# A two-layer hybrid decoder step: quartered first loads on two queues, a shorter table stage, small loads behind the weights, attention squares block by block

## The chip, the cores and the metric

One NeuronCore of a Trainium2 chip. Its engines work side by side and wait for each other by semaphores: TensorE (PE, matrix products), VectorE (DVE), ScalarE (ACT), GpSimd (POOL) and SyncE (SP, which here issues DMAs). The metric is the device time of one launch in microseconds (us), all inputs in the chip's memory; smaller is better.

## The reference

One inference step of two layers on 256 prompt tokens and 64 sample tokens (8 sequences of 8), all in fp32, model width 1024:

```python
x = x + 0.5 * swiglu(rms_norm(x, lw['ffn1_norm']), lw['ffn1_w_gate'], lw['ffn1_w_up'], lw['ffn1_w_down'])
mix, new_k, new_v, h_last = token_mixer(rms_norm(x, lw['mix_norm']), lw, h0, cache_k, cache_v)
x = x + mix
x = x + 0.5 * swiglu(rms_norm(x, lw['ffn2_norm']), lw['ffn2_w_gate'], lw['ffn2_w_up'], lw['ffn2_w_down'])
gate = jax.nn.sigmoid((rms_norm(x, lw['ple_norm']) @ lw['ple_w_gate']).astype(F32))
x = x + ((p @ lw['ple_w_proj']).astype(F32) * gate).astype(x.dtype)
```

`swiglu(h) = (silu(h @ w_gate) * (h @ w_up)) @ w_down` with an inner width of 2816. `token_mixer` projects to u, q, k, v; u goes through a state-space recurrence (S5: 32 groups of 16 channels, 64 complex states each, `h_t = Abar h_{t-1} + Bbar u_t`, then gelu and a gate), q, k, v through sliding-window attention with sinks; both results are normalised on their own (`rms_norm`), joined and projected by `w_out`. `Abar` and `Bbar` come from `exp(lam * dt)`. A last `rms_norm` ends the step. Outputs are y, the key/value windows and the final states.

## The kernel before

All 320 tokens stand in the free dimension: x is eight tiles `x[m]` of 128x320 (`xa`). Every fp32 product is made of three fp32r products (`mm3`, L178): the weight is split in a rounded part `wh` and the rest `wl`, the activations likewise in `big` pairs (`Norm.cut`, L218: ACT makes the rounded part L225, DVE the rest L226), and each 128-row step issues h·xh (L182), h·xl (L183) and lo·xh (L184).

**Weights** stream through `wfetch` (L150): SP loads a raw tile of up to 128x1024 (`wr`, 4 buffers), ACT copies it to fp32r (`wh`, L163), DVE subtracts (`wl`, L164); 4 buffers of each, three split weights kept ahead of the matmuls. For the very first weight the load and the cuts are made in two halves (`HEAD`).

**Norms** run late: matmuls work on the unnormalised x times the gain, and the result is scaled by r afterwards. `Norm.stat` makes squares and adds them (ACT L210 or POOL L212; sums by DVE or POOL, L216), `finish` adds over the partitions with three small matmuls (L244), DVE forms the mean `ms` (L247), POOL takes the power -0.5 (L249), and after `LATER` further matmuls PE spreads r over the partitions (L267) and DVE copies it.

**Head.** SP issues two tiles of x, the parameters `prm`, the two halves of the first gate weight, three tiles of x, the first up weight, three tiles of x, then the next weights. ACT and DVE cut x; POOL and ACT make the squares of all eight tiles. Block m=0 of the first FFN multiplies k-steps 0 to 6 and then 7 (`KCUT`) with either weight; `finish` comes after the third of such groups in general, and after the fifth here (FAFTER), which is m=1's gate product.

**FFN.** The inner width goes in two halves (12 and 10 blocks of 128). Each block m is a gate group into PSUM pool "pc" and an up group into "pt", 24 matmuls each; then eight down-projection blocks `mo` per half, of 36 matmuls with two 768-column weights in the first half and of 30 with two 640-column weights in the second. A second-half block ends with `fd` (L334), the addition to x (L335) and `post`, which cuts x for the next norm, squares it and adds the square.

**Table stage.** `prep(l)` (L378) is a generator of the state-space tables: powers of `Abar`, the B tables (L489, L493; transposed on PE into `wbd`), the C tables (L521, L525; `wcd`, and with matmuls the kernel taps `ktd`, copied into the triangular `ttd`, of which everything is first filled with zeros from a 128x1024 tile, 2 MB a layer, L385), and the tables of powers over chunks `ect`, `est`, `dec` (`er`, `us`, `uc`: L558 to L570; doubling L579 to L584; one step of normalising to modulus one, L590 to L595; L597). `ffn` takes one step of it after each of its 22 blocks and 16 down-projection blocks (`step`, L145), which also waits in program order for the last weight cut and load issued. `prep(0)` runs beside ffn1 of layer 0, `prep(1)` beside ffn2 of layer 0. prep(0) has 36 steps before, prep(1) fewer since its zero fills are prep(0)'s.

**Mix.** The mixer projects, runs the recurrence in chunks and the attention in prompt blocks (`Prompt`, one for each m, results to `ya[:, m, 0:256]`) and sample blocks, in a written-out order; `attn_norm` (L929) makes the four whole squares of `ya` and finishes, `ssm_norm` does the same for the recurrence. The loads of the state h0 (L689) and of the layer's embedding pT (L970) are issued wherever SP is free: at 20.50 and 20.97 us.

Instructions that no data ties together are placed by a scheduler that orders each engine's queue by estimated times; `tc.issue_after(i)` forbids it to place anything in its scope ahead of i.

## Time and profile before

| | |
|---|---|
| median of 3 runs | 1286.86 us (1286.62 to 1287.45) |
| the profiled execution | 1286.57 us |
| its span in the trace | 1284.8 us |
| mean granted clock of TensorE | 0.995 |
| PE busy | 1257.4 us, 98%, 9153 instructions |
| DVE, ACT, POOL busy | 911.0, 598.9, 81.5 us |
| moved by DMA | 210.62 MB, mean 164 GB/s |

All times count from the start of the span; some 1.8 us of the run's time lie around it. "Busy" of PE includes matmuls that run at the throttled clock. "x 9153" counts instructions. An entry such as `PE pt L184 <- DVE wl L164` reads: PE's instruction of line 184 that writes a tile `pt` had to wait for DVE's instruction of line 164 that writes `wl`. Queue rows (SPq) are the issue of a DMA, not its transfer. Matmuls overlap, so a matmul's duration (0.31 us) is longer than its distance to the next.

### The profile page before, as it was taken

How to read it: one execution, taken by the hardware profiler on the slowest of the kernel's cores; microseconds unless marked ns; L12 is line 12 of the kernel's file. 1: busy time of each engine (PE TensorE's matmuls, PEld its weight loads, DVE VectorE, ACT ScalarE, POOL GpSimd, SP SyncE). 2: the span in 40 equal slices, each digit the busy share in tenths (PEclk: the TensorE clock that was granted, in tenths of full speed). 3: DMA queues.
4: the chain of work that ended last, by engine and by line, in shares of the span. 5: the costliest groups of instructions: out<-in, count | busy, mean ns of one | idle time of the engine just before them, and what ended most of it. 6: DMA issues, size and time to landing. Idle time of an engine off the chain costs nothing.

```text
span 1284.8 us, 22994 instructions
## 1 busy us (share of the span) xinstructions
PE 1257.4 (98%) x9153; PEld 1231.1 (96%) x9153; DVE 911.0 (71%) x1609; ACT 598.9 (47%) x984; POOL 81.5 (6%) x96
## 2 busy tenths in 40 slices
PE   7999999899999999999999999999999999999996
PEld 7999999898899999999999999999888999999996
DVE  6588776978786878788785555557877755555575
ACT  5443433455764443344653333345476543333454
POOL 4300002001004000010000000000000000000000
PEclk9999999999999999999999999999999999999998
DMA  7836666354254468654444454345432444454351
GB/s 251 314 125 204 240 208 212 120 197 144 76 192 147 150 194 256 219 189 141 166 174 151 129 154 174 136 115 188 164 106 99 147 151 135 142 180 141 113 174 41
DMA packets 74620, 210.62 MB, mean 164 GB/s; under 512 B 8545, under 2 KB 18497, under 8 KB 74481
## 3 DMA queue, kind: packets, MB, share of 16 engines
q1 hardware_dynamic: 72560, 203.22, 47.8%
q0 software_dynamic: 1664, 5.28, 1.3%
q8 instruction: 72, 1.18, 0.4%
q10 hardware_dynamic: 288, 0.66, 0.1%
q14 instruction: 36, 0.29, 0.1%
HBM read 191.78 MB, written 19.69 MB: 165 GB/s over the span
## 4 chain that ended last, share of the span: by engine, by line
PE 89%; DVE 6%; issue 3%; ACT 1%; POOL 1%; DMA 0%; SPq 0%; POOLq 0%; DVEq 0%; ACTq 0%
PE pt L182 17%; PE pt L184 17%; PE pt L183 17%; PE pc L182 11%; PE pc L184 11%; PE pc L183 11%; DVE wl L164 2%; PE pa L872 1%; PE pa L500 1%; POOL r L249 1%; DVE s L704 0%; DVE s L703 0%; DMA xa<-xT 0%; PE pa L883 0%; PE pa L244 0%
## 5 line engine op out<-in xcount | busy, mean ns | idle before, releaser
L163 ACT ACTIVATE wh<-wr 128x1024 fp32r<-128x1024 f32 (+3 forms) x365 | 350.9, 963 | 556.3 <-issue 302.0
L184 PE MATMUL pt<-big,wl 128*128 128x320 f32 x1584 | 492.6, 311 | 4.3 <-DVE wl L164 4.3
L182 PE MATMUL pt<-big,wh 128*128 128x320 f32 x1584 | 493.4, 312 | 0.0
L183 PE MATMUL pt<-big,wh 128*128 128x320 f32 x1584 | 492.2, 311 | 0.0
L164 DVE TENSOR_TENSOR wl<-wr,wh 128x1024 fp32r<-128x1024 f32 (+3 forms) x365 | 403.1, 1107 | 100.5 <-ACT wh L163 98.5
L182 PE MATMUL pc<-big,wh 128*128 128x320 f32 x992 | 310.7, 314 | 6.7 <-ACT wh L163 6.0
L183 PE MATMUL pc<-big,wh 128*128 128x320 f32 x992 | 308.8, 312 | 0.0
L184 PE MATMUL pc<-big,wl 128*128 128x320 f32 x992 | 308.2, 311 | 0.0
L184 PEld LDWEIGHTS pt<-big,wl 128*128 128x128 f32 x1584 | 298.8, 189 | 6.0 <-DVE wl L164 5.5
L183 PEld LDWEIGHTS pt<-big,wh 128*128 128x128 f32 x1584 | 299.1, 189 | 0.5
L182 PEld LDWEIGHTS pt<-big,wh 128*128 128x128 f32 x1584 | 298.8, 189 | 0.7 <-issue 0.4
L182 PEld LDWEIGHTS pc<-big,wh 128*128 128x128 f32 x992 | 187.2, 189 | 9.6 <-ACT wh L163 6.2
L183 PEld LDWEIGHTS pc<-big,wh 128*128 128x128 f32 x992 | 187.1, 189 | 1.2 <-DVE big L226 1.2
L184 PEld LDWEIGHTS pc<-big,wl 128*128 128x128 f32 x992 | 187.2, 189 | 0.6 <-issue 0.3
L291 DVE TENSOR_TENSOR fa<-pt,ft 128x320 f32<-128x320 f32 x88 | 43.0, 489 | 91.0 <-PE pt L184 90.5
L288 DVE TENSOR_TENSOR ft<-pc,r 128x320 f32<-128x320 f32 x88 | 42.6, 488 | 53.6 <-PE pc L184 53.5
L334 DVE SCALAR_TENSOR_TENSOR fd<-pt,r 128x320 f32<-128x320 f32 x64 | 31.3, 490 | 31.6 <-PE pt L184 31.6
L249 POOL TENSOR_TENSOR r<-ms,mhalf 107x3 f32<-107x3 f32 x13 | 17.1, 1319 | 565.0 <-DVE ms L247 565.0
L225 ACT ACTIVATE big<-xa,prm 128x320 fp32r<-128x320 f32 x64 | 35.3, 559 | 31.4 <-DVE xa L335 17.4
L295 ACT ACTIVATE big<-fa 128x320 fp32r<-128x320 f32 x88 | 40.2, 459 | 14.6 <-DVE fa L291 14.5
L289 ACT ACTIVATE ft<-ft 128x320 f32<-128x320 f32 x88 | 40.0, 458 | 13.1 <-DVE ft L288 13.0
L226 DVE SCALAR_TENSOR_TENSOR big<-xa,prm,big 128x320 fp32r<-128x320 f32 x64 | 37.9, 599 | 8.4 <-ACT big L225 8.4
(246 smaller groups left out, 904.6 us busy)
## 6 DMA issues: line engine op xcount, KB each, us to landing
wr<-f1u SPq DMA_DIRECT2D x44, 512.0 KB, 3.2
wr<-f2g SPq DMA_DIRECT2D x44, 512.0 KB, 3.3
wr<-f2u SPq DMA_DIRECT2D x44, 512.0 KB, 3.3
wr<-f1g SPq DMA_DIRECT2D x43, 512.0 KB, 3.3
wr<-f1d SPq DMA_DIRECT2D x32, 384.0 KB, 3.1
wr<-f2d SPq DMA_DIRECT2D x32, 384.0 KB, 3.1
wr<-f1d SPq DMA_DIRECT2D x32, 320.0 KB, 2.9
wr<-win SPq DMA_DIRECT2D x20, 512.0 KB, 3.8
```

What stands on the lines that cost most here:

```text
L163: S.activation(h[:, c], raw[:, c], AF.Copy)
L164: i = V.tensor_tensor(lo[:, c], raw[:, c], h[:, c].bitcast(F32), op=OP.subtract)
L182: PE.matmul(ps, h[:, c], xh, start=start and k == 0, stop=False)
L183: PE.matmul(ps, h[:, c], xl, start=False, stop=False)
L184: PE.matmul(ps, lo[:, c], xh, start=False, stop=stop and k == n - 1)
L225: S.activation(h, src, AF.Copy, scale=g)
L226: V.scalar_tensor_tensor(lo, src, g, h.bitcast(F32), op0=OP.mult, op1=OP.subtract)
L288: V.tensor_tensor(t, pg, r, op=OP.mult)
L289: S.activation(t, t, AF.Silu)
L291: V.tensor_tensor(a, pu, t, op=OP.mult)
L295: S.activation(h, a, AF.Copy)
L334: V.scalar_tensor_tensor(t, pd, 0.5, r, op0=OP.mult, op1=OP.mult)
```

## The change

1. **Head.** `prm` is loaded first. x comes in quarters of two tiles (three on ACT's queue, the last on SP), and the first gate and up weights in quarters of 256 columns on SP; ACT and DVE cut tile, weight quarters, tile. Block m=0 goes by two k-steps, alternating both weights. Before any data, PE multiplies zeros 14 times (`NWARM`). The squares of x move behind m=0 and from POOL to ACT and DVE. Block m=2 uses the PSUM pool "po" for its gate product.
2. **Table stage.** The chunk tables (`er`, `us`, doubling) come right after the powers, and the normalising to modulus one is applied to the single first column before the doubling. The C tables come next, then the copies to `ttd`, then the B tables. The triangle's zeros are now 112 zero columns of `ktd` (240 wide), so that the copies have one shape and carry the zeros; the 2 MB fills go. prep(0) has 32 steps.
3. **Small loads.** h0 and pT are issued behind the last weight load issued (`later_load`).
4. **Attention squares.** Each prompt block squares its 256 columns and adds them when it is done; the sample columns of all four are squared at the end.
5. `LATER` is 18 instead of 22, and the spread of r may not be placed ahead of the 18th matmul. The `hold` argument of `finish` is not used by any caller.

```diff
-HEAD = 2
-LATER = 22
+NWARM = 14
+LATER = 18
...
+    headdma = []
+    nc.sync.dma_start(prm, I["prm"])
+    for q in range(4):
+        (S if q < 3 else nc.sync).dma_start(xa[:, 2 * q : 2 * q + 2], I["xT"][:, 2 * q : 2 * q + 2])
+        for raw, src in zip(first, firstw):
+            headdma.append(nc.sync.dma_start(raw[:, 256 * q : 256 * q + 256],
+                                             src[:, 256 * q : 256 * q + 256]).ins)
...
+    pz = pst("po")
+    for _ in range(NWARM):
+        PE.matmul(pz[:, :T], zr_[:, :P], zr_, start=True, stop=True)
...
+    def later_load(out, src):
+        with tc.issue_after(lastdma[-1]):
+            nc.sync.dma_start(out, src)
...
             if waiting:
                 waiting[0][0] -= 3
                 if waiting[0][0] <= 0:
-                    waiting.pop(0)[1]()
+                    with tc.issue_after(mm.ins):
+                        waiting.pop(0)[1]()
...
-                    for k0, k1 in ((0, KCUT), (KCUT, 8)):
+                    ks = (0, 2, 4, 6, 8) if head else (0, KCUT, 8)
+                    for k0, k1 in zip(ks, ks[1:]):
...
+                    if head:
+                        groups = 4
+                        for k in range(8):
+                            pre.stat(x[k])
                 else:
-                    for tag in ("pc", "pt"):
+                    for tag in ("po" if head and m == 2 else "pc", "pt"):
...
-            zt = wpool.tile([P, 1024], F32, name=nm("wr"), tag="wr", bufs=4)
-            PO.memset(zt, 0.0)
-            for ll in range(L):
-                nc.sync.dma_start(tt_d[ll].rearrange("p (b c) -> p b c", b=4),
-                                  zt.unsqueeze(1).to_broadcast([P, 4, 1024]))
-                yield
...
+        if l == 0:
+            zt = auxt("sx", [P, 4, 112])
+            PO.memset(zt, 0.0)
+            for ll in range(L):
+                nc.sync.dma_start(kt_d[ll].rearrange("(p b) c -> p b c", b=4)[:, :, 0:112], zt)
+            yield
...
+        V.tensor_tensor(t, uc, uc, op=OP.mult)
+        V.tensor_tensor(er, us, us, op=OP.mult)
+        V.tensor_tensor(t, t, er, op=OP.add)
+        V.tensor_scalar(t, t, -0.5, 1.5, op0=OP.mult, op1=OP.add)
+        V.tensor_tensor(ct_[:, :, 1], uc, t, op=OP.mult)
+        V.tensor_tensor(sn_[:, :, 1], us, t, op=OP.mult)
...
-            PO.dma_start(dst[:, :, i * 16 :], src[:, :, : (8 - i) * 16])
+            PO.dma_start(dst, src[:, :, (7 - i) * 16 : (7 - i) * 16 + P])
...
-        for c0 in (0, 16):
-            cc, ss = ct_[:, :, c0 : c0 + 16], sn_[:, :, c0 : c0 + 16]
-            q1, q2 = auxt("s", [P, G, 16]), auxt("p", [P, G, 16])
-            V.tensor_tensor(q1, cc, cc, op=OP.mult)
-            V.tensor_tensor(q2, ss, ss, op=OP.mult)
-            V.tensor_tensor(q1, q1, q2, op=OP.add)
-            V.tensor_scalar(q1, q1, -0.5, 1.5, op0=OP.mult, op1=OP.add)
-            V.tensor_tensor(cc, cc, q1, op=OP.mult)
-            V.tensor_tensor(ss, ss, q1, op=OP.mult)
...
+        def attn_stat(m):
...
+            if m is not None:
+                sq = na.acc if hold["acc"] else sm.tile([P, T], F32, name=nm("sq"), tag="sq", bufs=2)
+                S.activation(sq[:, 0:TP], ya[:, m, 0:TP], AF.Square)
+                if not hold["acc"]:
+                    V.tensor_tensor(na.acc[:, 0:TP], na.acc[:, 0:TP], sq[:, 0:TP], op=OP.add)
+                return
+            sq = sm.tile([P, 4, 64], F32, name=nm("sq"), tag="sq", bufs=2)
+            S.activation(sq, ya[:, :, TP:T], AF.Square)
...
         def attn_norm():
-            for m in range(4):
-                na.stat(ya[:, m, :])
...
+    for q in range(4):
+        pre.cut(2 * q, x[2 * q])
+        for raw, (h, lo) in zip(first, wready):
+            wsplit(h, lo, raw, slice(256 * q, 256 * q + 256))
+        pre.cut(2 * q + 1, x[2 * q + 1])
```

Where the order moves, first on PE at the start of the program, before the change (`pc` gate product, `pt` up product, `big` a part of x):

```order
L182 MATMUL pc_182<-big_110,wh_119 128x320
L183 MATMUL pc_182<-big_111,wh_119 128x320
L184 MATMUL pc_182<-big_110,wl_120 128x320
L182 MATMUL pc_182<-big_110,wh_119 128x320
L183 MATMUL pc_182<-big_111,wh_119 128x320
L184 MATMUL pc_182<-big_110,wl_120 128x320
L182 MATMUL pc_182<-big_110,wh_119 128x320
L183 MATMUL pc_182<-big_111,wh_119 128x320
```

and after it, the products on zeros ahead:

```order
L105 MATMUL po_102<-zr 128x320 x14
L206 MATMUL pc_194<-big_146,wh_142 128x320
L207 MATMUL pc_194<-big_147,wh_142 128x320
L206 MATMUL pt_195<-big_146,wh_144 128x320
L207 MATMUL pt_195<-big_147,wh_144 128x320
L208 MATMUL pc_194<-big_146,wl_143 128x320
L206 MATMUL pc_194<-big_146,wh_142 128x320
L208 MATMUL pt_195<-big_146,wl_145 128x320
L206 MATMUL pt_195<-big_146,wh_144 128x320
L207 MATMUL pc_194<-big_147,wh_142 128x320
L208 MATMUL pc_194<-big_146,wl_143 128x320
L207 MATMUL pt_195<-big_147,wh_144 128x320
```

The first weight's whole run of k-steps has become an alternation of both weights.

On DVE in the last down-projection blocks of ffn1 of layer 0, before (`fd` and `xa` are a block's own result, `ect` and `est` the chunk tables):

```order
L335 TENSOR_TENSOR xa<-xa,fd_2675 128x320
L580 TENSOR_TENSOR s_2684<-est_2527 128x480
L581 TENSOR_TENSOR p_2685<-ect_2526,est_2527 128x480
L226 SCALAR_TENSOR_TENSOR big_2515<-xa,prm,big_2514 128x320
L216 TENSOR_TENSOR acc_2518<-acc_2518,sq_2680 128x320
L582 TENSOR_TENSOR p_2686<-est_2527,ect_2526 128x480
L583 TENSOR_TENSOR ect_2526<-s_2683,s_2684 128x32x15
L584 TENSOR_TENSOR est_2527<-p_2685,p_2686 128x32x15
L164 TENSOR_TENSOR wl_2697<-wr_2694,wh_2696 128x640
L164 TENSOR_TENSOR wl_2718<-wr_2715,wh_2717 128x640
L334 SCALAR_TENSOR_TENSOR fd_2736<-pt_2693,r_306 128x320
L590 TENSOR_TENSOR s_2744<-ect_2526 128x512
```

and after:

```order
L172 TENSOR_TENSOR wl_2656<-wr_2653,wh_2655 128x640
L255 SCALAR_TENSOR_TENSOR big_2610<-xa,prm,big_2609 128x320
L172 TENSOR_TENSOR wl_2686<-wr_2683,wh_2685 128x640
L370 SCALAR_TENSOR_TENSOR fd_2674<-pt_2631,r_335 128x320
L371 TENSOR_TENSOR xa<-xa,fd_2674 128x320
L172 TENSOR_TENSOR wl_2707<-wr_2704,wh_2706 128x640
L255 SCALAR_TENSOR_TENSOR big_2610<-xa,prm,big_2609 128x320
L245 TENSOR_TENSOR acc_2613<-acc_2613,sq_2679 128x320
L172 TENSOR_TENSOR wl_2737<-wr_2734,wh_2736 128x640
```

The table steps have left this place; weight cuts and a block's own operations stay.

On PE at the attention's norm in layer 0's mix, before (L244 the sum over partitions, L267 the spread of r):

```order
L244 MATMUL pa_4032<-ones,acc_4021 107x1 x3
L183 MATMUL pc_4109<-big_2994,wh_3965 128x320
L184 MATMUL pc_4109<-big_2993,wl_3966 128x320
L182 MATMUL pc_4109<-big_2993,wh_3965 128x320
L267 MATMUL pa_4077<-ident,r_698_4038 128x107 x3
```

and after, where two of the three L273 stand 14 matmuls further ahead and this is the third:

```order
L207 MATMUL pc_4091<-big_3017,wh_3862 128x320
L273 MATMUL pa_4059<-ones,acc_3629 107x1
L208 MATMUL pc_4091<-big_3016,wl_3863 128x320
L206 MATMUL pc_4091<-big_3016,wh_3862 128x320
L207 MATMUL pc_4091<-big_3017,wh_3862 128x320
L208 MATMUL pc_4091<-big_3016,wl_3863 128x320
L298 MATMUL pa_4098<-ident,r_696_4065 128x107 x3
```

Between the last sum and the spread stand four matmuls, before as after.

## Rows read from the trace of the kernel before

**Rows 1.** Page, busy us (share of the span) and instructions of each engine.

```profile
PE 1257.4 (98%) x9153; PEld 1231.1 (96%) x9153; DVE 911.0 (71%) x1609; ACT 598.9 (47%) x984; POOL 81.5 (6%) x96
```

**Rows 2.** PE's waits: what waits, for what; us in total, times, longest us.

```profile
PE pc L182 <- ACT wh L163: 6.0, 1, 6.0
PE pt L184 <- DVE wl L164: 4.3, 4, 1.9
```

**Rows 3.** Stretches: us, busy us (count) per engine; granted clock, DMA share, GB/s.

```profile
232.00:241.20 9.20, 5.98 (x39) 5.45 (x38) 9.20 (x18) 2.81 (x5) 0.00 (x0) 1.00 0.21 72
241.20:244.60 3.40, 3.40 (x16) 3.40 (x15) 3.40 (x8) 1.55 (x3) 0.00 (x0) 0.52 0.60 195
244.60:250.50 5.90, 5.90 (x41) 5.90 (x41) 5.90 (x12) 2.61 (x5) 0.00 (x0) 0.99 0.42 114
```

**Rows 4.** PE by time: start, duration, line, operation, count.

```profile
19.08 0.47 PE L183 MATMUL pt<-big,wh 128*128 128x320 f32 x1
19.35 0.38 PE L184 MATMUL pt<-big,wl 128*128 128x320 f32 x1
...
24.40 0.64 PE L244 MATMUL pa<-ones,acc 128*107 128x1 f32 x6
...
28.50 0.44 PE L267 MATMUL pa<-ident,r 107*128 107x107 f32 x3
```

**Rows 5.** Stretches of the head, columns as in rows 3.

```profile
6.00:9.00 3.00, 2.26 (x7) 1.63 (x7) 1.48 (x4) 1.34 (x3) 0.66 (x1) 1.00 1.00 378
9.00:12.30 3.30, 3.30 (x9) 2.39 (x10) 3.30 (x4) 2.74 (x6) 3.14 (x5) 1.00 1.03 420
```

**Rows 6.** PE near 240 us, by time; in brackets idle time and releaser.

```profile
233.70 0.41 PE L184 MATMUL pt<-big,wl 128*128 128x320 f32 x1 [1.34 <-DVE wl L164]
...
240.24 0.41 PE L184 MATMUL pt<-big,wl 128*128 128x320 f32 x1 [1.88 <-DVE wl L164]
...
251.73 0.41 PE L184 MATMUL pt<-big,wl 128*128 128x320 f32 x1 [0.90 <-DVE wl L164]
```

**Rows 7.** DVE in the same stretch, by time.

```profile
241.24 0.68 DVE L590 TENSOR_TENSOR s<-ect 128x512 f32<-128x512 f32 x1
```

**Rows 8.** DMA issues up to 12 us: count, KB each, median us to landing.

```profile
xa<-xT SPq DMA_DIRECT2D x2, 480.0 KB, 6.4
```

**Rows 9.** SyncE's queue by time: start, duration of the issue.

```profile
3.54 0.43 SPq L1026 DMA_DIRECT2D xa<-xT  x1
```

**Rows 10.** ACT by time in the head.

```profile
4.06 1.01 ACT L225 ACTIVATE big<-xa,prm 128x320 fp32r<-128x320 f32 x2 [1.82 <-DMA prm<-prm]
...
8.29 1.47 ACT L225 ACTIVATE big<-xa,prm 128x320 fp32r<-128x320 f32 x3 [0.71 <-DMA xa<-xT]
```

**Rows 11.** Durations by line: ns min/median/max, first and last start, forms.

```profile
L163 ACT ACTIVATE wh<-wr x365: 629/1059/1065, 5.3 to 1257.8; 128x1024 fp32r<-128x1024 f32 x118, 128x768 fp32r<-128x768 f32 x32, 128x640 fp32r<-128x640 f32 x32, 128x512 fp32r<-128x512 f32 x1
...
L164 DVE TENSOR_TENSOR wl<-wr,wh x365: 679/1218/1883, 6.0 to 1262.0; 128x1024 fp32r<-128x1024 f32 x118, 128x768 fp32r<-128x768 f32 x32, 128x640 fp32r<-128x640 f32 x32, 128x512 fp32r<-128x512 f32 x1
```

**Rows 12.** Durations of the norm's power on POOL, columns as in rows 11.

```profile
L249 POOL TENSOR_TENSOR r<-ms,mhalf x13: 848/1065/1807, 25.3 to 1276.0; 107x3 f32<-107x3 f32 x13
```

**Rows 13.** Durations of the C tables' products on DVE, columns as in rows 11.

```profile
L521 DVE TENSOR_TENSOR s<-sx,vc x16: 748/752/759, 148.6 to 527.8; 128x576 f32<-128x576 f32 x16
```

**Rows 14.** A stretch of the first half's down-projection blocks, columns as in rows 3.

```profile
110.00:121.00 11.00, 11.00 (x79) 11.00 (x78) 9.04 (x14) 4.20 (x6) 0.00 (x0) 1.00 0.76 238
```

**Rows 15.** The power of dt on POOL, by time.

```profile
49.63 5.43 POOL L402 TENSOR_TENSOR dt<-econ,lam 128x32 f32<-128x32 f32 x1 [3.08 <-DMA lam<-lam]
```

**Rows 16.** Page, DMA issues: count, KB each, median us from issue to landing.

```profile
wr<-f1u SPq DMA_DIRECT2D x44, 512.0 KB, 3.2
```

**Rows 17.** PE at the spreads of the two norms of the mix, layer 0.

```profile
349.74 0.49 PE L267 MATMUL pa<-ident,r 107*128 107x107 f32 x3 [0.86 <-POOL r L249]
...
361.70 0.49 PE L267 MATMUL pa<-ident,r 107*128 107x107 f32 x3 [0.69 <-POOL r L249]
```

**Rows 18.** A stretch of the mix, layer 0, columns as in rows 3.

```profile
320.00:332.00 12.00, 11.79 (x135) 10.41 (x131) 10.69 (x28) 10.51 (x34) 1.06 (x2) 1.00 0.49 175
```

More of the change, by code (lines that the diff above doesn't have):

```diff
@@ L1 @@
 import math
[L2 removed]
+from contextlib import ExitStack, nullcontext
 import numpy as np
@@ L181, in mm3 @@
             c = slice((off + k) * P, (off + k + 1) * P)
-            PE.matmul(ps, h[:, c], xh, start=start and k == 0, stop=False)
-            PE.matmul(ps, h[:, c], xl, start=False, stop=False)
-            PE.matmul(ps, lo[:, c], xh, start=False, stop=stop and k == n - 1)
+            with tc.issue_after(held[0]) if held else nullcontext():
+                PE.matmul(ps, h[:, c], xh, start=start and k == 0, stop=False)
+                PE.matmul(ps, h[:, c], xl, start=False, stop=False)
+                mm = PE.matmul(ps, lo[:, c], xh, start=False, stop=stop and k == n - 1)
+            if held:
+                held[1] -= 3
+                if held[1] <= 0:
+                    held.clear()
             if waiting:
@@ L243, in finish @@
                 for i, a in enumerate(sums):
-                    PE.matmul(ps[:SN, c : c + 1], a[:, t0 : t0 + SN], ones, start=i == 0,
+                    mm = PE.matmul(ps[:SN, c : c + 1], a[:, t0 : t0 + SN], ones, start=i == 0,
                               stop=i == len(sums) - 1)
@@ L260, in later @@
                 then(r)
-            waiting.append([LATER, later])
+            waiting.append([hold or LATER, later])
+            if hold:
+                held[:] = [mm.ins, hold]
         def spread(self, r4):
@@ L269, in spread, with ffn @@
             return pr[:, :T]
-    def ffn(l, idx, pre, post, side=None, after=3):
+    def ffn(l, idx, pre, post, side=None, after=3, head=False):
         xs = pre.pairs()
```

208 lines of the change are left out of this document (104 added, 104 removed).

## The prediction

> **What bounds the kernel now.** I read the page's busy times first: PE is busy 98% of the span [rows 1]. Only two things can move the time, then: the stretches in which PE waits, and those in which it runs at the lower clock. So the list of PE's waits came next [rows 2]: 6.0 us once for the first cut weight, 4.3 us in four waits for `wl`. The busy share hides the clock. In the steady state 128x320 matmuls follow each other by 0.146 us (41 in 5.90 us from 244.6 on [rows 3]); in the head the spacing is 0.27 us up to the matmul at 19.35 us [rows 4]. The stretch from 241.2 to 244.6 us is spaced like that for all but its first matmuls, and there the granted clock is 0.52 (16 matmuls in 3.40 us [rows 3]); so I read the head as the 1.2 GHz level although its own clock column reads 1.00 [rows 5]. PE had run from 15.9 to 19.35 us without a gap when it rose.
>
> The head's loss is one subtraction. The ones-matmul of the first norm (L244), at 24.40 us [rows 4], stands behind 72 matmuls: 48 for m=0, 24 for m=1. At 0.146 they take 10.5 us, so 13.9 us are lost by then.
>
> The other loss is the end of ffn1 of layer 0. From 232 to 241.2 us DVE is busy for the whole 9.20 us and PE for 5.98; at 241.2 PE's clock falls to 0.52 [rows 3]. The three long waits there are 1.34, 1.88 and 0.90 us, all for `wl` [rows 6]; in between DVE runs the steps of `prep(0)`, the largest 0.68 us each [rows 7].
>
> **The head.** The change splits the first 2.4 MB in quarters (of x two tiles, of two weights 256 columns each), issues three quarters of x on ACT's queue, runs 14 matmuls on zeros meanwhile, and cuts and multiplies quarter by quarter.
>
> What arrives when: before, x and the first two weights are in flight together, and DMA is busy all the time from 6 to 12.3 us at 378 to 420 GB/s [rows 5]. The two 480 KB pieces of x take 6.4 us from issue to landing [rows 8]; the second, issued at 3.54 [rows 9], lands near 10.7 (the median of two is their mean; the first is there at 8.29, when ACT's next cut starts [rows 10]). The bytes that m=0 needs are the same after the change, and DMA was the limit, so the last quarter lands at 9.8 to 10.7 us; I take 10.2. The first quarter with the parameters is 0.64 MB, about what had landed before when ACT cut the weight that PE's first matmul waited for until 6.0 [rows 2], so its matmuls can start near 6.3.
>
> Work per quarter: ACT cuts two tiles (three took 1.47 [rows 10], so 0.98) and twice 256 columns (0.63 at the least, for 512, and 1.06 for 1024 [rows 11], so about 0.42 each): 1.8 us. DVE has about the same. A quarter of the loads comes every 1.6 us, 12 matmuls at 0.146 are 1.75 us. ACT ends the last quarter near 12.0, then cuts m=1's first weight until 13.1; DVE's `wl` of 1.22 us [rows 11] follows until 14.3. Three matmuls of m=1 can go before that, the other 45 take 6.6 us: 96 matmuls are done at 20.9. Before, they were done at 28.50 with 0.50 us for L244 among them: 28.0. That is 7.1 us, if the clock is high by then.
>
> The norm costs something back. The order puts only 9 matmuls (1.3 us) between the new L273 and L298, where 24 stood between L244 and L267. The power on POOL takes 0.85 to 1.81 us [rows 12], and two short DVE and PE steps stand around it, so PE waits 0.3 to 1.0 us; I take 0.6. The squares move from POOL to ACT and DVE: 8 of 0.47 and 7 adds of 0.48. ACT's row from 12.0 us, five weight cuts and eight squares, is 9.0 us and ends at 21; the L273 comes behind 103 matmuls, at about 21.9. That fits with 0.9 us to spare. With the clock: the 14 zero matmuls take 14 x 0.267 = 3.7 us from about 1.4 us, without a gap, and PE stands idle for about 1 us before the first quarter. If the clock is up from there, nothing is lost; if it rises at 9, 10 matmuls are done by then, m=0 ends at 14.5 instead of 14.1, and 0.2 to 0.4 go. I take **6.3 us** for the head (7.1 - 0.6 - 0.2); bounds 3.2 (rise at 14 us, and 1 us for the norm) and 7.4 (last quarter at 9.8, 0.3 for the norm). ACT's three issues cost nothing: before, it waits 1.82 us for the first x [rows 10], and three issues at 0.43 [rows 9] are 1.3.
>
> The Trainium skill, DMA: Bandwidth & Descriptors, section "Issuing engines are not separate DMA queues", speaks against this part: DMAs of several engines run on the same 16 engines, and a second issuer saves only sequencer time. The bandwidth rows from 6 to 12.3 us agree; by it alone the last quarter would still land at 10.7 and the head would give 0.5 us less.
>
> **The tail of ffn1.** Before, `prep(0)` needs 36 steps, and the powers' tables (L579 to L597) are the last ones. They fall on the second half's down-projection blocks, where `post` adds a cut and an addition and DVE has only 30 x 0.146 = 4.4 us a block. Without them a block costs DVE two `wl` of 0.74 and four operations of 0.40 to 0.48: 3.2 us. After the change prep needs 32 steps and ends with block 1 of that half; the order shows nothing but a block's own work from there. So the waits go. Start to start, the three are 1.5, 2.0 and 1.1 us beyond 0.146 (the idle time and about 0.15 of slow restart); 13 matmuls at 0.267 cost 1.6, and about 0.7 lie in smaller gaps: **6.9 us**. I take 6.6, since at block 0 and 1 the last `es` step still shares DVE; bounds 4.0 and 6.9.
>
> What the tables cost in their new place: the normalising of 12 operations on 512 columns (0.68 each, 7 us) becomes one of 32 columns before the doubling. The doublings stand in the gate/up groups, at 48 matmuls a step. The C tables (L521, 0.75 us each [rows 13]) move to the first half's blocks: six on a gb, 4.5 us on two blocks, beside 2.1 us of own work a block; in 110 to 121 us the B tables of 0.68 each leave DVE 9.04 of 11 us busy and PE without a gap [rows 14]. With 0.5 more a gb that is 9.6 of 10.7. Three cut weights stand ahead, so I cost this at nothing; with that cover gone it is what exceeds it, below 0.5 us a gb.
>
> **The zero fill and the queue.** Two 2 MB zero fills go, two of 0.23 MB come, and these wait on SP for a POOL memset that stands behind the norm's power and the one of dt, 5.43 us [rows 15]. SP holds the weights of m=5 behind it until about 30 us. PE needs these at 6.9 + 240 x 0.146 = 42 us, and load (3.2 us [rows 16]), cut and subtraction take 5.5: nothing, with 6 us to spare.
>
> **The mix.** PE waits 0.86 us at 349.74 and 0.69 at 361.70 for `r` [rows 17]. The attention squares now come block by block, but the third ones-matmul of that norm still stands four matmuls ahead of L298, as L244 did before L267, and for the other norm nine instead of ten. So most of both waits stays. Three squares of 256 columns (about 0.4) and their adds move into 320 to 332 us, where ACT is busy 10.51 of 12 and PE loses 0.2 already [rows 18]; four squares and three adds leave the stretch ahead of the norm. I take 0.1 us lost a layer, **-0.2 us** in all; bounds -1.2 and +2. h0, pT and LATER at 18 have one answer, nothing: ACT's copy of h0 now waits for a load issued behind a weight, with two cuts queued behind that copy, but three cut weights stand ahead of PE, 6.6 us or more; pT's weight is issued later than pT; and 18 matmuls (2.6 us) still cover the power.
>
> **Sum.** 6.3 + 6.6 - 0.2 = 12.7 us off the profiled run of 1286.57 (span 1284.8 and 1.8 around it): 1273.9. The median lies 0.29 above that run, so 1274.1.
>
> **Rivals.**
> (A) The clock stays low in the head. Zero matmuls may not be what raises it, or the idle 1 us lowers it again: at 240.24 us two gaps of 1.34 and 1.88 were followed by the low level. For it: before, PE worked from 6 us with gaps and stayed low until 19.35. Against: it rose there after a stretch without gaps, and the quarters keep PE full (at 0.267, 12 matmuls are 3.2 us, a quarter 1.8). If it rises at 13, m=0 ends at 16.4, the head gives 4.2 and the time is 1276.2; if at 19, the head gives 1.5: 1278.9.
> (B) The quarters load worse. Nine loads of 128 to 320 KB where five were; if the bytes come at 330 GB/s and not at 400, the last quarter lands at 12 and the head gives 4.5: 1275.9. The rate of the first 6 us, with a load's start in it, speaks for it, the full rate beside halves of 256 KB against.
> (C) The C tables wake a wait in the first half, as L164 has it in the tail. Half the tail's gain gone: 1277.4. For it DVE's 9.6 of 10.7; against it the three weights ahead.
> (D) Slower: SP held behind the zero fill. Each us by which the memset comes after 36.5 us stalls PE for one; from 49 us on all gain is gone. At 54 us it would be 1274.1 + 17.5 = 1291.6. The power of dt would have to take 25 us instead of 5.4, or lam, which it reads, come that late.
>
> **How the numbers follow.** Forecast 0.50, A 0.20, B 0.10, C 0.13, D 0.05, and 0.02 for losses in the mix beyond its bound. About 0.2% (2.6 us) is what a measurement of this kernel can tell from no change. All of A, B and C leave more than that, unless two meet at their worst: same 0.06, slower 0.05, faster 0.89. The range takes the bounds: 1286.9 - 7.4 - 6.9 - 2 = 1270.6 at one end; at the other 1280, A's late rise beside a mix at its bound.
>
> **What would show it.** In the profile of after: spacing 0.146 from the first quarter on, no gap over 0.3 us until 14 us, and the new L273 near 22; three `wl` waits of over 0.5 us gone between 225 and 260 us, with DVE below 85% there; the waits for r still about 0.8 and 0.7 us; no new `wl` wait between 90 and 135 us. The prediction is wrong if the head spacing stays 0.267 beyond 14 us, if SP's weight for m=5 lands after 40 us, or if L206 waits for a cut in the first half.

## The result, and the profile of the changed kernel

The changed kernel takes 1276.91 us (median; 1276.52 to 1277.02), the kernel before 1287.15 in the same session: a ratio of 0.9921, 95% interval 0.9909 to 0.9934. The prediction was 1274.1, range 1270 to 1280. The gain is 10.2 us where 12.7 were forecast, and it is not made up as forecast.

From the page, the engines' busy time and the chain that ended last:

```profile
PE 1257.2 (99%) x9167; PEld 1230.7 (97%) x9167; DVE 901.4 (71%) x1611; ACT 602.0 (47%) x995; POOL 69.0 (5%) x85
...
PE 93%; DVE 3%; issue 2%; ACT 1%; DMA 0%; POOL 0%; POOLq 0%; SPq 0%; DVEq 0%; ACTq 0%
```

PE's busy time is that of [rows 1] to 0.2 us, with 14 products more; DVE's share of the chain fell from 6% to 3%.

Both kernels execute the same 9153 matrix instructions on PE, leaving out the 14 products on zeros. So the start of PE's n-th instruction can be compared in the two traces, which tells at each place how far ahead the changed kernel is:

| place (time in the kernel before) | lead, us | this part, us | forecast |
|---|---|---|---|
| 43 us, behind the first norm | 4.5 | head 4.5 | 6.3 |
| 260 us, end of layer 0's first FFN | 11.3 | table stage 6.8 | 6.6 |
| 370 us, behind layer 0's mix | 10.3 | mix -1.0 | -0.1 |
| 890 us, start of layer 1's mix | 10.2 | prep(1) 0.0 | 0.0 |
| 1000 us, behind it | 9.3 | mix -1.0 | -0.1 |
| last matmul | 9.3 | 0.0 | 0.0 |

The table stage came out as forecast, the head 1.8 us short, and the mix lost 2.0 us where 0.2 were forecast. The two profiled executions differ by 9.6 us (1286.57 and 1276.93); the 0.4 that the table lacks lie behind the last matmul. (Inside a part the lead is no measure, since the order of the instructions differs there.)

**Tail of ffn1.** About the same times as in [rows 3], by the same columns (the program is 4.5 us further on at the start of this stretch and 11.3 at its end):

```profile
225.00:232.00 7.00, 7.00 (x50) 7.00 (x49) 5.05 (x10) 3.49 (x6) 0.00 (x0) 1.00 0.64 228
232.00:241.20 9.20, 9.20 (x65) 9.20 (x64) 7.18 (x14) 5.19 (x9) 0.00 (x0) 1.00 0.65 214
241.20:250.00 8.80, 8.80 (x62) 8.80 (x61) 7.97 (x13) 5.98 (x9) 0.00 (x0) 1.00 0.62 223
```

PE is busy throughout, DVE for 20.2 of 25.0 us, and the waits for `wl` of [rows 2] and [rows 6] are gone. The place that took over the C tables is at its limit, without a loss:

```profile
102.00:113.00 11.00, 11.00 (x88) 10.61 (x87) 10.97 (x17) 3.38 (x4) 0.00 (x0) 1.00 0.68 215
```

DVE is busy for 10.97 of 11 us, PE for all of them.

**Head.** PE by time, to be held against [rows 4]; a stretch of equal rows is one row with a count:

```profile
1.77 4.10 PE L105 MATMUL po<-zr 128*128 128x320 f32 x14 [1.77 <-DVE zr L102]
5.94 0.64 PE L206 MATMUL pc<-big,wh 128*128 128x320 f32 x1
...
10.54 0.47 PE L206 MATMUL pc<-big,wh 128*128 128x320 f32 x1
10.80 0.43 PE L206 MATMUL pt<-big,wh 128*128 128x320 f32 x1
11.07 0.32 PE L207 MATMUL pt<-big,wh 128*128 128x320 f32 x1
...
16.10 0.41 PE L206 MATMUL pt<-big,wh 128*128 128x320 f32 x1
16.35 0.31 PE L208 MATMUL pc<-big,wl 128*128 128x320 f32 x1
...
24.26 0.70 PE L273 MATMUL pa<-ones,acc 128*107 128x1 f32 x6
...
26.47 0.49 PE L298 MATMUL pa<-ident,r 107*128 107x107 f32 x3
```

The spacing is 0.27 us up to 10.80 and 0.15 from 11.07. PE had no gap from 7.33 on when it rose. The last of m=0's 48 products starts at 15.49, the 96th product at 22.80. The sum of the squares (L273, behind 104 products) starts at 24.26, where about 21.9 was forecast, and the spread of r (L298) follows nine products later.

The duration of a product tells the clock as its spacing does: a product of 128x320 lasts 0.47 us at the long spacing and 0.31 at the short one. Another execution of the same head, that of the whole attention squares below, had the clock up before its first product on data:

```profile
1.77 3.91 PE L105 MATMUL po<-zr 128*128 128x320 f32 x14 [1.77 <-DVE zr L102]
5.89 0.41 PE L206 MATMUL pc<-big,wh 128*128 128x320 f32 x1 [0.22 <-ACT wh L171]
6.15 0.31 PE L207 MATMUL pc<-big,wh 128*128 128x320 f32 x1
```

**SP and POOL.** SP's issues, and POOL's two rows that the zero fill waits for:

```profile
2.60 0.45 SPq L95 DMA_DIRECT2D wr<-f1u  x1
3.98 0.33 SPq L95 DMA_DIRECT2D wr<-f1g  x1
...
7.55 0.33 SPq L181 DMA_DIRECT2D wr<-f1g  x1
...
32.27 1.28 SPq L438 DMA_DIRECT2D ktd<-sx  x2
```

```profile
26.38 5.44 POOL L427 TENSOR_TENSOR dt<-econ,lam 128x32 f32<-128x32 f32 x1
31.75 0.48 POOL L436 MEMSET sx<- 128x448 f32 x1
```

The fill is issued at 32.27 us, where 30 was expected; the weights behind it land at 38.7 and 40.0, and nothing on PE waits for them. Rival D stayed away.

**Mix.** PE's waits there, from the list for the whole program, and one of the four at L699 by time:

```profile
PE pa L298 <- POOL r L278: 3.0, 3, 1.3
...
PE pt L827 <- DVE s L816: 1.2, 2, 0.6
PE pa L699 <- DVE big L682: 0.9, 4, 0.3
```

```profile
268.83 0.62 PE L699 MATMUL pa<-ident,big 128*40 128x128 f32 x4 [0.28 <-DVE big L682]
```

L298 waits three times, 1.3 at the last norm of the program and 0.87 in either mix; L827 (the flip of the scaled scores) waits 0.6 a layer and L699 (the transposes of the recurrence's input) up to 0.28, and neither of these two waited as long before. In the kernel before, the spread of r waited five times:

```profile
PE pa L267 <- POOL r L249: 4.3, 5, 1.3
```

So the second wait of [rows 17], 0.69 us at the recurrence's norm, is gone in both layers. The waits listed over one mix add up to 2.75 us in layer 0, before as after: what was lost at L827 and L699 was won at that norm and in a smaller wait. The 1.0 us a layer by which the mix is longer lie in PE's busy time there, in longer distances between matmuls, which the list doesn't count. A list of waits alone would have shown no loss.

### The profile page after: what moved, and what is told of

The parts are those of the page before. It is cut to its first block, busy times and chain, and to the rows that moved or that the text cites. A ratio compares the mean times of both kernels' runs of the same rounds, so it can differ in the third digit from the quotient of the medians.

```text
span 1275.2 us, 23019 instructions
## 1 busy us (share of the span) xinstructions
PE 1257.2 (99%) x9167; PEld 1230.7 (97%) x9167; DVE 901.4 (71%) x1611; ACT 602.0 (47%) x995; POOL 69.0 (5%) x85
## 4 chain that ended last, share of the span: by engine, by line
PE 93%; DVE 3%; issue 2%; ACT 1%; DMA 0%; POOL 0%; POOLq 0%; SPq 0%; DVEq 0%; ACTq 0%
PE pt L206 18%; PE pt L207 18%; PE pt L208 17%; PE pc L206 11%; PE pc L207 11%; PE pc L208 11%; PE pa L923 1%; PE pa L623 1%; PE po L836 0%; PE pa L273 0%; DVE wl L172 0%; PE pt L827 0%; DVE s L734 0%; DVE s L733 0%; PE pa L934 0%
## 5 line engine op out<-in xcount | busy, mean ns | idle before, releaser
L206 PE MATMUL pc<-big,wh 128*128 128x320 f32 x984 | 307.5, 313 | 0.1
L207 PE MATMUL pc<-big,wh 128*128 128x320 f32 x984 | 305.2, 310 | 0.0
L208 PE MATMUL pc<-big,wl 128*128 128x320 f32 x984 | 305.1, 310 | 0.0
L327 DVE TENSOR_TENSOR big<-fa,big 128x320 fp32r<-128x320 f32 x88 | 42.7, 486 | 1.1 <-ACT big L326 1.1
```

The lines of the kernel that those rows point to most:

```text
L206: PE.matmul(ps, h[:, c], xh, start=start and k == 0, stop=False)
L207: PE.matmul(ps, h[:, c], xl, start=False, stop=False)
L208: mm = PE.matmul(ps, lo[:, c], xh, start=False, stop=stop and k == n - 1)
L327: V.tensor_tensor(lo, a, h.bitcast(F32), op=OP.subtract)
```

## The experiments

Each kernel is the changed kernel with the edit named. The leads are those of the table above, against the kernel before, in one profiled execution: behind the head, for the table stage, and for both mixes. The first four kernels have the same head, so its 4.0 to 4.8 us are also what one execution differs from the next.

| edit | median, us | head | tables | mixes |
|---|---|---|---|---|
| none (the changed kernel) | 1276.9 | 4.5 | 6.8 | -2.0 |
| whole attention squares | 1276.3 | 4.2 | 6.8 | -1.0 |
| LATER at 22 | 1274.1 | 4.0 | 6.8 | +1.1 |
| both | 1275.2 | 4.8 | 6.8 | -0.1 |
| no zero products | 1282.1 | 2.8 | 6.8 | -2.0 |
| 22 zero products | 1277.3 | 4.4 | 6.8 | -2.0 |
| weights in halves | 1277.8 | 4.1 | 6.8 | -2.0 |
| small loads early | 1277.8 | 2.0 | 6.8 | -2.0 |
| old table stage | 1285.6 | 2.9 | -1.7 | -1.9 |
| old head | 1281.0 | 1.5 | 6.8 | -1.9 |
| LATER 22, late first sum | 1273.2 | 5.3 | 6.8 | +1.1 |
| as above, halves, 22 zero products | 1273.1 | 6.0 | 6.8 | +1.1 |
| as above, additions on POOL | 1272.6 | 6.0 | 6.8 | +1.9 |

A median holds besides some 0.5 us of change from execution to execution. One source is the last norm's ten sums behind PE's longest wait, of 2.5 us: they start 0.09 us apart in some executions and 0.18 in others, whatever the edit, and take nothing (the changed kernel, both edits together, weights in halves) to 0.9 us (late first sum) of the lead.

### Attention squares whole again

```diff
         def attn_norm():
+            for m in range(4):
+                na.stat(ya[:, m, :])
             na.finish(lambda ra: [na.cut(m, ya[:, m, :], ra) for m in range(4)])
```

(with the two calls of `attn_stat` taken out.)

> The changed kernel (1276.9 us) with the attention squares made as before, four whole squares when the attention norm starts. Theory: the block-wise squares and adds stand among the softmax steps on ACT and DVE, delay the scaled scores that PE flips (a new wait of 0.58 us a layer) and cost some 1.0 us in each layer's mix. Without them the mix gives back 2.0 us in all: 1274.9, and PE's wait at the flip for the scaled scores is below 0.1. Rival: the mix's loss comes from the pinned spread with 18 instead of 22 matmuls, or from the later loads: then the time stays at 1276.9 within 0.4 and the index-aligned loss from the start to the end of the mix stays at 1.0 us a layer.

Measured: 1276.31 us (1275.58 to 1276.88); the mixes lose 1.0 us instead of 2.0. The wait of 0.58 at L827 is gone, and that at the recurrence's norm is back with 0.83. So the squares account for half of the loss at most, and the theory that they are all of it fell. The wait for r at 0.86 stayed, which led to the next run.

### LATER at 22

```diff
-LATER = 18
+LATER = 22
...
-                    with tc.issue_after(mm.ins):
-                        waiting.pop(0)[1]()
+                    waiting.pop(0)[1]()
```

(The second part changes nothing: with 22 and with 18, the program's order on all engines is the same with or without it.)

> The changed kernel with LATER at 22 and the spread of r free to be placed, as before. Theory: the other half of the mix's loss (making the attention squares whole had given back 0.5 us a layer, not 1.0) comes from the earlier spread of the mix norm: it moves the first projections, so that PE reaches the transposes of the recurrence's input (L699) before DVE has evacuated them, four waits of 0.2 to 0.3 us. Then these waits fall to 0.1, the mix gives back 0.5 us a layer and the time is 1275.9. Rival: the spread's place is worth nothing in the mix, the L699 waits stay, 1276.9 within 0.4.

Measured: 1274.12 us (1273.15 to 1274.48), 2.8 us faster than the changed kernel and more than expected. The waits at L699 fell from 0.28 to 0.16 at most, which was the theory, but the larger part lies at the attention norm. There the changed kernel has, PE by time,

```profile
336.38 0.26 PE L273 MATMUL pa<-ones,acc 128*107 128x1 f32 x2
...
338.20 0.49 PE L298 MATMUL pa<-ident,r 107*128 107x107 f32 x3 [0.87 <-POOL r L278]
```

and with LATER at 22

```profile
336.55 0.26 PE L272 MATMUL pa<-ones,acc 128*107 128x1 f32 x2
...
338.38 0.49 PE L297 MATMUL pa<-ident,r 107*128 107x107 f32 x3
```

Its third sum comes at the same distance from the spread, 1.82 and 1.83 us, but in the first PE waits for 0.87 of these, in the second it works: six more products stand between. PE's list of waits says the same for the whole program:

```profile
PE pa L297 <- POOL r L277: 1.3, 1, 1.3
PE pt L826 <- DVE s L815: 1.2, 2, 0.6
```

One wait for r is left of three, that of the last norm.

### Both: whole squares and LATER at 22

> The changed kernel with both LATER at 22 and the four whole attention squares, as before the change; only LATER at 22 had given 1274.1, only the whole squares 1276.3. Theory: the two work together. Block by block the sums of the attention norm are ready early, and then the number of matmuls that its spread must wait for decides; with whole squares the third sum is late whatever that number, and PE waits 0.86 us for the power again. So here the mix takes as long as before the change (1.1 us more in all than with LATER at 22 alone): 1275.2. Rival: the two add up, the squares cost 0.5 us a layer at any LATER, and it is the fastest of the four, 1273.1.

Measured: 1275.18 us (1274.71 to 1275.66), the theory's number. The mixes stand at -0.1, as in the kernel before. PE by time at the attention norm:

```profile
336.05 0.72 PE L272 MATMUL pa<-ones,acc 128*107 128x1 f32 x6
...
338.18 0.49 PE L297 MATMUL pa<-ident,r 107*128 107x107 f32 x3 [0.86 <-POOL r L277]
```

The wait of 0.86 is back, that of [rows 17], and the other one there with 0.69. So the four combinations are: whole squares and 22, -0.1 us; whole and 18, -1.0; block by block and 22, +1.1; block by block and 18, -2.0. The squares block by block are worth 1.2 us where enough products stand before the spread, and cost 1.0 where they don't; in the medians it is 1.1 and 0.6. The 18 costs 3.1 us with the squares block by block and 0.9 with whole ones (2.8 and 1.1 in the medians). Neither number alone says what the two edits of the change do together.

### Small loads early again

```diff
     def later_load(out, src):
-        with tc.issue_after(lastdma[-1]):
-            nc.sync.dma_start(out, src)
+        nc.sync.dma_start(out, src)
```

> The changed kernel with the loads of h0 and pT free to be issued early. Theory: they cost and gain nothing where they are now: 1276.9 within 0.4, the mix as in the changed kernel. Rival: their late issue is what delays ACT and DVE at the start of the mix: then the stretch from 249 to 285 us is 0.5 us shorter a layer and the time 1275.9; or, early again, they take bandwidth in the head, where the next weights are awaited, and the time is up to 0.6 us longer.

Measured: 1277.75 us (1277.07 to 1279.43), 0.8 slower by the median, with ranges that hardly part (the changed kernel's ends at 1277.02); the mix unchanged, the head 2.5 us worse in the profiled execution, which was the slowest of the four. h0 and pT are issued at 8.42 and 8.90 us there, the weight for m=2's gate lands at 18.1 instead of 16.3, the sum of squares waits 1.3 us for DVE, and from 27.0 us on PE's spacing is 0.27 again for a while. So holding these loads back seems to have a worth, which I had put at nothing; its size is not shown by four executions.

### Zero products: none, and 22

```diff
-NWARM = 14
+NWARM = 22
```

(and, in the other kernel, the tile of zeros and the loop of products left out.)

> The changed kernel without the 14 products on zeros. In the changed kernel PE's spacing drops to 0.146 at 10.95 us, after it had worked without a gap from 7.33. Theory: the zero products, which ended with a short gap at 5.7 us, bought nothing; the clock rises between 10.5 and 11.5 us again and the time stays at 1276.9 within 0.4. Rival: they did raise the share of work that lets the clock rise; without them it rises at 14 us or later, m=0 ends 1.5 to 3 us later and the time is 1278.4 to 1280.

> The changed kernel with 22 products on zeros instead of 14, so that PE has no gap between 1.8 and 7.6 us, by when the first quarter is cut. Theory: the clock rises earlier than 10.95 (at 7.5 to 8), but the first FFN block then waits for its last quarter (landed 11.5 in the changed kernel) and m=1 for its weight (landed 13.7, wl ready at 16.0): the gain is at most 0.5 us, 1276.4. Rival: PE at the lower clock is the only limit of the head; then m=0 ends near 13.5 instead of 15.6 and the time falls by 2 us to 1274.9. Third: the clock rises at 10.95 as before, then PE does 8 fewer products of m=0 by then and the time is some 1 us longer, 1278.

Without them: 1282.07 us, executions from 1280.2 to 1282.5; the profiled one took 1280.3. Its clock rose at 11.12 us, near the 10.80 of the changed kernel, as the theory had it, but the time did not stay. PE by time around the first sum of squares:

```profile
24.02 0.69 PE L264 MATMUL pa<-ones,acc 128*107 128x1 f32 x6 [0.86 <-DVE acc L236]
...
26.00 0.49 PE L289 MATMUL pa<-ident,r 107*128 107x107 f32 x3 [0.73 <-POOL r L269]
```

The scheduler now put this sum behind 95 products and only three more before the spread; PE waits 0.86 us for DVE's last addition and 0.73 for r. So against the changed kernel's profiled execution the zero products show no effect through the clock; their absence shows through the order. That is 1.7 us of the 3.4 between the two profiled executions; 0.6 more lie in the last sums and 0.9 behind the last matmul. What makes three of the five executions 1.8 us slower still was not traced, and stays open: a later rise of the clock in these is not excluded.

With 22, the clock rises at 5.13 us and stays up; m=0's last product starts at 14.18 instead of 15.49, and then m=1 waits for its second weight, 0.7 us. The 96th product starts at 22.63, against 22.80: 1277.32 us (1276.99 to 1277.91), no gain. That is the first theory; the clock is not the only limit of the head.

The same shows between executions of one and the same head (but for two small loads in one). The first product that is shorter than 0.47 us starts at 10.80 (changed kernel), 10.57 (LATER at 22), 5.13 (whole squares), 5.40 (both), 6.48 (small loads early) and 4.60 us (LATER 22, late first sum), and the 96th product at 22.80, 22.53, 22.33, 22.48, 22.69 and 22.48. So the 14 products on zeros did raise the clock early in four of these six executions, and four to six microseconds of an earlier rise are worth half a microsecond at most. (The 7.3 us that an expectation below names is where the unbroken run at the short spacing begins; the clock was up before it.)

### The first weights in halves

```diff
-        for raw, src in zip(first, firstw):
-            headdma.append(nc.sync.dma_start(raw[:, 256 * q : 256 * q + 256],
-                                             src[:, 256 * q : 256 * q + 256]).ins)
+        for raw, src in zip(first, firstw) if q % 2 == 0 else ():
+            headdma.append(nc.sync.dma_start(raw[:, 256 * q : 256 * q + 512],
+                                             src[:, 256 * q : 256 * q + 512]).ins)
```

> The changed kernel with the first two weights loaded in halves of 512 columns instead of quarters (x still in quarters, the cuts still in quarters). Theory: the head is bound by its loads, not by PE's clock: in the changed kernel SP's sixth issue stands until 3.98 us for the first of eight transfers in flight to land, the rate falls to 235 GB/s between 9 and 12 us, and m=1's weight lands at 13.7 and is ready at 16.0. With five issues on SP fewer transfers wait, the weight lands by 12.3, wl is ready by 14.6, and the 72nd product starts 1.0 to 1.5 us earlier than 19.3; at the sum of the squares some of it is lost again (it waits for DVE): 1276.0 to 1276.5. Rival: the size of the pieces is not what delays m=1's weight; it lands within 0.5 us of 13.7 and the time stays at 1276.9.

The loads did what the theory said. The changed kernel and then this one, from 9 to 12 us, columns as in rows 3 (the last is GB/s):

```profile
9.00:12.00 3.00, 3.00 (x16) 3.00 (x16) 2.84 (x8) 2.54 (x8) 0.00 (x0) 1.00 0.92 235
```

```profile
9.00:12.00 3.00, 3.00 (x15) 3.00 (x15) 3.00 (x8) 3.00 (x9) 0.00 (x0) 1.00 0.92 374
```

235 GB/s became 374, and m=1's weight landed at 11.3 us instead of 13.7, when ACT starts to cut it in the changed kernel:

```profile
13.70 1.06 ACT L171 ACTIVATE wh<-wr 128x1024 fp32r<-128x1024 f32 x1 [1.27 <-DMA wr<-f1g]
```

But the time went to 1277.80 us (1277.74 to 1277.98), more than either theory had: the larger first pieces came later, PE had gaps until 8.0, its clock rose at 11.08, and m=0's last product started at 16.16. From there PE had no gap up to the 96th product at 23.20: with the loads mended the clock was the limit. The rates hold in the other traces: over the same three microseconds 201 to 300 GB/s in nine executions with quarters, 365 to 375 in three with halves. In the three microseconds before those, the quarters ran at 315 to 360. So the small pieces are not slow as such, and which of the five loads in flight from 9 to 12 us holds up the others is not shown. The Trainium skill, DMA: Bandwidth & Descriptors, section "Measured (HBM→SBUF, 128 partitions, SWDGE, issued from GpSimd)", says to batch loads and that small ones lose bandwidth; the two rows agree in direction, for kernels with pieces of 128 and of 256 KB.

### The old table stage, and the old head

In the first, `prep` is that of the kernel before with its `ktd` of 128 columns; in the second, the loads, the cuts, the squares and the order of m=0 are those of the kernel before.

> The changed kernel with the table stage of the kernel before (its order, its normalising on 512 columns, its 2 MB zero fills). Theory: the table stage alone gave the 6.8 us by which the changed kernel is ahead between 225 and 257 us, so the time goes up by 6.8 to 1283.7 and the three waits for wl of over 0.8 us are back. Rival: part of them would have gone anyway, since the head now leaves all queues earlier and the loads of the tail come differently; then the time is 1280 or less.

> The changed kernel with the head of the kernel before (its loads in two or three tiles and whole weights from one queue, no zero products, squares on POOL, block 0 in its old order). Theory: the parts add up, the new head is worth 4.5 us up to the first norm and the time is 1281.4. Rival: they don't add up; the old table stage cost the new head 1.4 us and another 1.8 between 43 and 85 us, which the old head hid, so with the new table stage the old head also runs better than it did before (one raw buffer more for weights) and is worth less: 1279.9 or less.

With the old table stage: 1285.63 us (1285.29 to 1287.84), not 1283.7; the profiled execution took 1287.16, 1.5 above the median. In it the new head keeps only 2.9 us of its lead, and the tables cost 8.5 us (6.8 and 1.7) instead of 6.8. The waits for weights:

```profile
PE pt L208 <- DVE wl L172: 5.6, 3, 2.4
...
PE pc L208 <- DVE wl L172: 1.4, 1, 1.4
```

The three of 5.6 us are those of the tail. The 1.4 is new: two 2 MB fills are issued at 28.98 and 30.30 us, the weight issued behind them lands at 45.85, and PE waits for its cut:

```profile
31.43 1.33 SPq L181 DMA_DIRECT2D wr<-f1g  x1
...
49.02 0.42 PE L208 MATMUL pc<-big,wl 128*128 128x320 f32 x1 [1.41 <-DVE wl L172]
```

The kernel before had the same fills, issued at 27.13 and 28.44 us, and no such wait; its PE came 2.9 us later to this place. So the old head seems to have hidden them, and removing the fills is a part of the gain that the difference of the two profiles does not show. The 1.6 us that the head lost come earlier than the fills and have another cause: PE waited 0.80 and 0.72 us for m=1's weights, and from 16.7 to 20.2 us the spacing was 0.27 again. They may be this execution's alone: 6.8 and 1.7 nearly make up the 8.7 between the medians.

With the old head: 1281.00 us (1280.85 to 1281.76); the sum of the parts had given 1281.4. The head is not quite that of the kernel before, though: its clock rises at 15.7 us instead of 19.35, and it is 1.5 us ahead. In the trace the new head is worth 3.0 us, not 4.5; the medians differ by 4.1, and 0.6 of the 3.9 between the profiled executions lie in the last sums, which vary.

### A late first sum, then all together, then the additions on POOL

```diff
-FAFTER = (5, 3, 4)
+FAFTER = (7, 3, 4)
...
-            waiting.append([hold or LATER, later])
+            waiting.append([hold or self.later or LATER, later])
...
+    pre.later = 12
     side = prep(0)
```

> LATER at 22, and in the head the sum of the first norm is asked for after 120 products (m=2's gate) instead of 72, its spread 12 products later. Theory: the wait for the sums (0.6 to 1.3 us in the executions seen) and the one for the power go, and nothing else in the head moves, since block m=3 needs its PSUM buffer only at product 144: 1.2 us less than with LATER at 22 alone, 1272.9. Rival: the late r makes m=3 wait for a free buffer; then the same time is lost 3 us later, 1274.1 or more.

> As the one before, with the first weights in halves and 22 zero products, so that neither the loads of m=1 nor the clock binds alone. Theory: the head has two limits that take turns (the clock rises at 10.6 to 11.1 us or at 7.3 from one execution to the next, with no gain in the 96th product from the earlier rise, since m=1's weight comes at 13.7; with the weights in halves it comes at 11.3, with no gain since that run's clock rose at 11.1). With both mended the 96th product starts by 21.3 instead of 22.5 and the time is 1.2 us below the one before: 1271.7. Rival: a third limit stands right behind (ACT and DVE, which cut m=1's weight after all the quarters); the 96th product stays near 22.5 and the time at 1272.9.

Late sum: 1273.24 us (1272.91 to 1273.93), and the waits for the sum and for r are gone from the head (lead 5.3 instead of 4.0). With the halves and 22 zero products besides: 1273.13 us (1272.54 to 1273.58). The clock rises at 7.53, m=1's weight lands at 11.1, PE has no gap left behind 8 us, and the 96th product starts at 21.72, 0.76 earlier; the theory had 21.3. The run before had its clock up at 4.60 and waited 0.72 us for m=1's second weight, so the 0.76 are the loads'. The lead grows by 0.75 in the trace, the median by 0.1, which the spread of the executions does not tell apart: the product came near the theory, the time stayed where the rival had it.

```diff
-                    V.tensor_tensor(na.acc[:, 0:TP], na.acc[:, 0:TP], sq[:, 0:TP], op=OP.add)
+                    PO.tensor_tensor(na.acc[:, 0:TP], na.acc[:, 0:TP], sq[:, 0:TP], op=OP.add)
```

> The fastest kernel so far (LATER at 22, the first norm's sum after 120 products, first weights in halves, 22 zero products; 1273.1) with the blocks' additions of attention squares on POOL instead of DVE. Theory: DVE's addition of 0.42 us between the scaled scores is what makes PE wait 0.58 us a layer at the flip (L827); on POOL that wait falls below 0.2 and the time to 1272.3. Rival: ACT's square, not DVE's addition, delays the softmax, or POOL's addition slows DVE beside it; then the wait stays above 0.4 and the time at 1273.1 or above.

In the changed kernel DVE makes its addition (L781) between two scaled scores, and PE waits for the softmax behind them:

```profile
308.62 0.56 DVE L805 SCALAR_TENSOR_TENSOR s<-pt,maskp 128x384 f32<-128x384 f32 x1
309.09 0.42 DVE L781 TENSOR_TENSOR acc<-acc,sq 128x256 f32<-128x256 f32 x1
309.43 0.55 DVE L805 SCALAR_TENSOR_TENSOR s<-pt,maskp 128x384 f32<-128x384 f32 x1
```

```profile
311.83 0.41 PE L827 MATMUL pt<-ident,s 128*128 128x128 f32 x2 [0.58 <-DVE s L816]
```

On POOL:

```profile
309.81 0.41 PE L827 MATMUL pt<-ident,s 128*128 128x128 f32 x2 [0.31 <-DVE s L816]
```

The wait falls to 0.31 (0.2 was expected) and the time to 1272.61 us (1272.40 to 1273.05), 4.3 us below the changed kernel: 0.989 of the kernel before, interval 0.9874 to 0.9907. It is the lowest median found; its range overlaps that of the version before it, while the mixes gain 0.8 us in the trace.

## Why the prediction was right or wrong

**The tail: right.** 6.6 us forecast, 6.8 measured; the three waits are gone, the C tables cost nothing in their new place, and DVE there is nearer to its limit (10.97 of 11) than the 9.6 of 10.7 that I had worked out.

**The head: mechanism right, size off by 1.8 us.** The step that failed is "what arrives when". I took the last quarter at 10.2 us and m=1's `wl` at 14.3; they came at 11.5 and at 16.0. The later quarter cost ACT little: it ended the quarters at 12.4 where I had 12.0. But I had it cut m=1's first weight at once, without a term for that weight's load; ACT waited 1.27 us and began at 13.70. I had costed SP's issues at 0.43 us each and left out what they wait for. The program gives its loads eight semaphores in turn, so the ninth load waits for the first to land, the tenth for the second, and so on. SP's sixth issue stands from 3.05 to 3.98, when the first quarter of x has landed at 3.96; the eighth to tenth issue at 5.46, 6.01 and 6.43 follow landings at 5.45, 6.00 and 6.41, and m=1's weight, issued at 7.55, one at 7.54. Ten issues at the spacing of the first four (0.46) would have let it go at 5.4. The program's order has these waits, in the rows for SP:

```
5 L95 DMA wr_84<-f1u 128x256
6 L95 DMA wr_83<-f1g 128x256 [waits DMAHW0_49]
7 L95 DMA wr_84<-f1u 128x256 [waits DMAHW1_49]
```

The second half of the same step is the rate: 323, 348 and 235 GB/s over the three stretches of 3 us from 3 to 12, where I had counted on 400. That is rival B, to which I had given one chance in ten: its quarter at 12 us and 4.5 us for the head are near what came. Rival A, the late clock, came too in the profiled execution (10.8 us), but the executions with a rise at 4.6 to 6.5 us show that it decides nothing by itself: they wait 0.45 to 0.75 us for m=1's second weight instead. In the changed kernel's trace the 96 products are done at 22.95 us, where the forecast had 21.1 (20.9, and 0.2 for the clock), and the norm costs 0.55 us where 0.6 were forecast. But the sum, which I had called covered with 0.9 us to spare, waits 0.8 us for DVE in two other executions of this head, and that is the larger part of what the late sum gave back (1.3 us).

**The mix: wrong.** I forecast -0.2 us; the measured -2.0 lies beyond my bound of -1.2, to which I had given 0.02. I gave LATER at 18 "one answer, nothing", because 18 products, 2.6 us, cover the power. They do where they stand behind the sum. At the attention norm the count starts when the sum is asked for, and the scheduler placed the third sum 14 products later; of the 18, four were left. I had read these four in the order, "as before", and had concluded that the wait would stay as it was. It did, with 0.87 us; the step that failed is the one that put LATER at 18 at nothing. I compared with the old kernel and did not ask what the old number would have given with the new squares. The mixes would have gained 1.1 us. The runs put 3.1 us on the 18 and show that most of it hangs on the squares' new place, since with whole squares it costs 0.9. The wait accounts for 0.87 of the 1.5 us a layer and the waits at L699 for 0.3; the rest lies in distances between matmuls. That the second wait of [rows 17] would stay too was wrong: it is gone with the squares block by block, and back without them.

**The zero fill and SP: right** (32.3 us where 30 was expected, no wait). **Small loads: probably wrong** in being put at nothing, by 0.8 us of the median, which four executions do not make sure.

That the time lies in the range is in part luck: both sizes failed in the same direction, by 1.8 us each, and the range reached so far up for a head with a late clock, which was not the reason.

## What to carry to other kernels

A wait that is counted in instructions ahead is only as good as the place at which the count begins: when work is moved forward, set the count again, and read in the order how many instructions are left between producer and consumer, for the old value as well as for the new. Before loads are cut smaller, count how many may be in flight and who waits for the slot of whom; the first pieces come earlier and the next whole load later. In a stretch with two limits that lie close together (a clock and a load), mending one alone showed nothing here or a loss, and parts that each hide the other's cost do not add up.

## What was not expected of the hardware

The time at which PE's clock rises differs from execution to execution of the same head by 6 us (4.60 to 10.80), although PE is without a gap from 1.8 to 5.1 us at least and has gaps of at most 0.7 us from there on in all of them; the executions with the late rise did not have the longer gaps. With 22 products on zeros, from 1.77 us on without any gap, it rose at 5.13 in one execution, at 7.26 and 7.53 in two others. DMA's rate from 9 to 12 us was 201 to 300 GB/s in the executions whose first weights came in pieces of 1 KB a partition, and 365 to 375 with pieces of 2 KB, with the engines of the DMA as busy (0.92 in the two rows shown).
